# The second feed-forward product by 26 chained block products instead of two times seven

## The chip, the cores and the metric

The kernel runs on one core of a Trainium2 chip. The metric is the device time of one execution in microseconds (us). Three executions of the kernel before gave 2304.38, 2305.03 and 2305.79 us; the median, 2305.03, is the time before.

## What is computed

One layer of a decoder: 2048 tokens of width 1024, a mixer (gated linear attention beside dilated windowed attention), then a feed-forward block of width 4096, all in float32. The change touches only the feed-forward block:

```python
nm = rmsnorm(h, mlp_norm_g[l])
a = jnp.square(jax.nn.relu(jnp.einsum('bsd,df->bsf', nm, w_ff1[l])))
h = h + jnp.einsum('bsf,fd->bsd', a, w_ff2[l])
...
return rmsnorm(h, final_norm_g)
```

So `a` is 2048 x 4096, `w_ff2` is 4096 x 1024, and the product of the two, added to `h` and normalised, is the output.

## The kernel before, in words

**One float32 product on TensorE.** Each float32 operand is split into a high part in the matmul's type and a low part with the rest (`split`, L408 to L410: ScalarE copies the high part, VectorE subtracts it to give the low part). `mm3` (L63 to L66) then issues three matmuls of 128x128 by 512 columns: high by high, low by high, high by low.

**The first product (FF1).** `product1` and `prep1` work through 2 halves of the tokens x 16 groups of 256 columns x 7 block products. A job is 12 matmuls into one PSUM bank. `prep1(at + 2)` makes the split weight block for the job two further on, in a ring of four. L1253 and L1254 apply ReLU and square. After the seventh job of a group, four sums of blocks (L1279 to L1282) are made on VectorE, and seven tiles of 128x512 go to the DRAM buffer `actD`, in the form in which the second product wants them. Seven 512-column pieces per group (X, c11 to c22, s2, s4) live in a double-buffered accumulator `acc1`. The transposed, split activations of a half fill 14 slots (`hb`); near job 106 of 224 `reload` brings in those of the other half, two more VectorE and ScalarE passes per `hb` pair.

**The second product (FF2).** It uses the same scheme of 7 products of 2x2 blocks, once for each half of the tokens: 14 phases. A phase has four PSUM banks (one for each 128 tokens) and 8 steps; a step takes 2 chunks of 128 inner columns, 24 matmuls. `load_a` brings 1 MB of activations for two steps, `prep_a` splits a step's 128x1024 of them (ring of 3, two steps ahead). `load_b`/`prep_b` bring and split the weights, subtracting a second block first where the product wants a difference (L1374); eight split weight tiles are kept, so that both halves use them. `taken` (L1400) adds a finished bank into the running sums (L1414), which start as `h`, and `output` (L1384) normalises a finished row block: squares on ScalarE (L1389), a multiply on GpSimd (L1391), one on VectorE (L1394), the scale on ScalarE (L1395), and the store. In the last phase the last three steps run bank by bank (L1504 on), so that each bank can be put out while the next one is multiplied.

**What sets the order.** A framework schedules: it puts the instructions into a fixed order on each engine and waits in them by semaphores. An engine runs its own instructions in that order. Nearly all DMAs are issued by SyncE's queue (SP). All large tiles come from one pool of 25 slots of 128x2112 float32; a new tile waits until a slot is free. PSUM has eight banks, named a (2), c (3), d (2), o (1).

Of the kernel before, what the change touches and what calls it, by code (L numbers as in the profile page):

```python
# [18 lines left out]
D = 1024  # L19
# [18 lines left out]

def emit(tc, a, stop=99):
# [23 lines left out]
    def mm3(out, sh, sl, mh, ml, first, last):  # L63
        T.matmul(out, sh, mh, start=first, stop=False)  # L64
        T.matmul(out, sl, mh, start=False, stop=False)  # L65
        T.matmul(out, sh, ml, start=False, stop=last)  # L66
# [80 lines left out]
    actD = dram.tile([7, 2, FF // 256, 128, 512], F32, name="actD")  # L147
    tD = dram.tile([2, FF // 256, 128, 512], F32, name="tD")
# [996 lines left out]
    gs = slot("gs")  # L1145
    gM, gF = gs[:, :D], gs[:, D:2 * D]
# [92 lines left out]

    def product1(at):  # L1240
        g, j = jobs1[at]
        half, gh = divmod(g, NP)
        if not acc1:
            acc = [slot("acc1") for _ in range(4)]
            acc1.extend(t[:, 512 * q:512 * q + 512] for t in acc for q in range(4))
        X, c11, c12, c21, c22, s2, s4 = acc1[7 * (g % 2):7 * (g % 2) + 7]
# [9 lines left out]
        def store(q, n, v):  # L1256
            q.dma_start(actD[n - 1, half, gh], v)
# [3 lines left out]
        elif j == 2:  # L1261
            V.tensor_tensor(c11, p, X, op=OP.add)
            square(c11)
            store(A, 1, c11)
        elif j == 6:
            V.tensor_tensor(X, p, X, op=OP.add)
            V.tensor_tensor(c12, X, c22, op=OP.add)
        elif j == 3:
            V.tensor_tensor(c12, p, c12, op=OP.add)
            square(c12)  # L1270
        else:
            V.tensor_tensor(X, p, X, op=OP.add)
            V.tensor_tensor(c21, c21, X, op=OP.add)  # L1273
            V.tensor_tensor(c22, c22, X, op=OP.add)
            square(c22)
            square(c21)
            store(SP, 4, c22)
            store(SP, 2, c21)
            V.tensor_tensor(X, c12, c22, op=OP.add)  # L1279
            V.tensor_tensor(s2, X, c11, op=OP.subtract)  # L1280
            V.tensor_tensor(c12, c11, c12, op=OP.subtract)
            V.tensor_tensor(s4, c21, s2, op=OP.subtract)  # L1282
            for n, v in ((5, X), (6, s2), (7, c12), (3, s4)):
                store(SP, n, v)
# [39 lines left out]
    order2 = (1, 2, 5, 6, 3, 4, 7)  # L1324
    phases = [(j, half) for j in order2 for half in range(2)]
    raw_a, comb_a, raw_b, comb_b, sums = [], [], [], [], {}

# [4 lines left out]
    def load_a(n):  # L1332

        if n < 4 * len(phases):
            j, half = phases[n // 4]
            if len(raw_a) < 2:
                raw_a.append(view(slot("ra"), (4, 512)))
            SP.dma_start(raw_a[n % 2], actD[j - 1, half, 4 * (n % 4):4 * (n % 4) + 4].rearrange("c p s -> p c s"))

    def prep_a(n):  # L1340

        if n >= 8 * len(phases):
# [3 lines left out]
        c = comb_a[n % 3]  # L1346
        split(c[:, 0], c[:, 1], raw_a[n // 2 % 2][:, n % 2 * 2:n % 2 * 2 + 2])
# [3 lines left out]
    def load_b(n):  # L1351

        if n >= 56:
            return
        j, c = order2[n // 8], 2 * (n % 8)
        if len(raw_b) < 2:
            raw_b.append(view(slot("rb2"), (2, 2, 512)))
        pairs2 = tD.rearrange("k c p s -> k p c s")
        of = {(k, m): w2[:, 2 * c + k:2 * c + k + 3:2, 512 * m:512 * m + 512] for k in range(2) for m in range(2)}
        kept = [pairs2[k][:, c:c + 2] for k in range(2)]  # L1360
        for at, v in enumerate({1: [of[0, 0]], 2: [of[1, 0]], 5: [of[0, 1], of[0, 0]], 6: [of[1, 1], kept[0]],
                                3: [of[1, 1]], 4: [of[1, 0], kept[1]], 7: [of[1, 1], of[0, 1]]}[j]):
            SP.dma_start(raw_b[n % 2][:, at], v)

    def prep_b(n):

        if n >= 56:
            return
        j, c = order2[n // 8], 2 * (n % 8)
# [194 lines left out]
```

## Time and profile before

| what | value |
|---|---|
| median of three runs | 2305.03 us |
| span of the profiled execution, first to last instruction | 2300.5 us |
| TensorE busy (matmuls) | 2281.5 us, 99% of the span |
| VectorE / ScalarE / GpSimd busy | 1534.2 (67%) / 1182.0 (51%) / 308.2 us (13%) |
| DMA, mean over the span | 199 GB/s |

The profile gives no total of its own for the profiled execution beyond its span; the median of the runs lies 4.5 us above that span. In the rows, PE is TensorE's matmuls, PEld its weight loads, DVE is VectorE, ACT is ScalarE, POOL is GpSimd and SP is SyncE's DMA queue. A row of the groups has the line, engine, operation, output and inputs, shapes and count; then busy time in us and the mean ns of one; then the idle time of that engine just before such instructions and what ended it. Records of consecutive instructions on one engine overlap a little, so the distance between two starts is shorter than a duration: matmuls of 512 columns have records of 389 ns and start every 0.23 us.

### The profile page before, as it was taken

Reading aid. Unit: us, or ns where it says so; the run is one execution under the profiler, and the core shown is the slowest. Engines: PE = TensorE matmul, PEld = TensorE weight load, DVE = VectorE, ACT = ScalarE, POOL = GpSimd, SP = SyncE. Lnnn points to the kernel's source line nnn. Section 1 sums busy time; section 2 is a strip of 40 time slices with the busy share of each in tenths; the row PEclk is TensorE's granted clock in tenths of the full one; section 3 lists DMA queues with packets and bytes.
Section 4 is the critical chain, followed back from the end, with each engine's and each line's share of the span. In section 5 each row is a group of like instructions: output and inputs, shape, how many; then the busy total and the mean of one; then the engine's idle time right before and its main releaser. Section 6 shows DMA issues by size and latency. Waiting matters only on the chain.

```text
span 2300.5 us, 34940 instructions
## 1 busy us (share of the span) xinstructions
PE 2281.5 (99%) x12700; PEld 1976.2 (86%) x12700; DVE 1534.2 (67%) x2845; ACT 1182.0 (51%) x2372; POOL 308.2 (13%) x394
## 2 busy tenths in 40 slices
PE   9999999999999999999999999999999999999998
PEld 8978998899999988888888888888888888888887
DVE  7787867767767685446777788777755446447444
ACT  6665536426877783335555566555544323225224
POOL 1210002024476671000000000000000100000002
PEclk9999999999999999999999999999999999999999
DMA  6467745776768765678544456444487477448543
GB/s 209 124 197 240 252 138 157 210 234 222 230 196 255 239 218 166 201 254 264 190 151 151 151 190 240 151 151 151 151 279 253 160 263 265 144 158 287 193 161 110
DMA packets 341806, 457.60 MB, mean 199 GB/s; under 512 B 18118, under 2 KB 214231, under 8 KB 336257
## 3 DMA queue, kind: packets, MB, share of 16 engines
q1 hardware_dynamic: 336878, 446.71, 60.0%
q10 hardware_dynamic: 4754, 8.66, 1.0%
q8 instruction: 100, 1.64, 0.3%
q14 instruction: 74, 0.60, 0.1%
HBM read 292.99 MB, written 167.02 MB: 200 GB/s over the span
## 4 chain that ended last, share of the span: by engine, by line
PE 52%; ACT 1%; DVE 0%; issue 0%; ACTq 0%
PE ps_c L65 6%; PE ps_c L66 6%; PE ps_c L64 6%; PE ps_a L66 4%; PE ps_a L65 4%; PE ps_a L64 4%; PE ps_d L64 4%; PE ps_d L66 4%; PE ps_d L65 4%; PE ps_o L66 2%; PE ps_o L65 2%; PE ps_o L64 2%; ACT scr L1389 0%; DVE hb L410 0%; ACT hb L409 0%
## 5 line engine op out<-in xcount | busy, mean ns | idle before, releaser
L410 DVE TENSOR_TENSOR ca<-ra,ca 128x1024 fp32r<-128x1024 f32 x112 | 138.0, 1232 | 171.3 <-ACT ca L409 171.2
L409 ACT ACTIVATE ca<-ra 128x1024 fp32r<-128x1024 f32 x112 | 117.9, 1053 | 229.9 <-PE ps_c L66 191.1
L409 ACT ACTIVATE w1comb<-w1raw 128x512 fp32r<-128x512 f32 x224 | 140.0, 627 | 153.6 <-PE ps_c L66 56.1
L1391 POOL TENSOR_TENSOR suma<-suma,gs 128x512 f32<-128x512 f32 x16 | 23.4, 1477 | 1393.6 <-ACT scr L1389 1393.6
L410 DVE TENSOR_TENSOR w1comb<-w1raw,w1comb 128x512 fp32r<-128x512 f32 x224 | 153.8, 689 | 50.5 <-ACT w1comb L409 50.4
L816 PE MATMUL ps_a<-v,pt 128*128 128x65 f32 x1200 | 178.4, 253 | 2.5 <-ACT pt L804 1.8
L788 ACT ACTIVATE pe<-pe,O 128x256 f32<-128x256 f32 (+1 forms) x384 | 156.6, 453 | 46.3 <-DVE O L787 42.8
L816 PEld LDWEIGHTS ps_a<-v,pt 128*128 128x128 f32 x1200 | 175.2, 195 | 3.6 <-ACT pt L804 2.1
L797 PE MATMUL ps_d<-ident,pe 128*128 128x128 f32 x600 | 159.3, 279 | 0.0
L787 DVE CUSTOM_DVE_ANT_0 pe<-ps_c,nb 128x256 f32<-128x256 f32 (+1 forms) x384 | 126.2, 360 | 40.9 <-PE ps_d L797 18.3
L209 ACT ACTIVATE wcomb<-wraw 128x512 fp32r<-128x512 f32 (+2 forms) x119 | 90.0, 757 | 99.0 <-PE ps_a L65 32.7
L409 ACT ACTIVATE cb<-rb 128x1024 fp32r<-128x1024 f32 x56 | 59.4, 1060 | 150.6 <-PE ps_o L65 115.0
L65 PE MATMUL ps_c<-hb,w1comb 128*128 128x512 f32 x336 | 130.8, 389 | 0.4 <-DVE w1comb L410 0.4
L64 PE MATMUL ps_c<-hb,w1comb 128*128 128x512 f32 x336 | 130.7, 389 | 0.0
L66 PE MATMUL ps_c<-hb,w1comb 128*128 128x512 f32 x336 | 130.7, 389 | 0.0
L64 PE MATMUL ps_c<-cb,ca 128*128 128x512 f32 x336 | 130.7, 389 | 0.0
L65 PE MATMUL ps_c<-cb,ca 128*128 128x512 f32 x336 | 130.7, 389 | 0.0
L66 PE MATMUL ps_c<-cb,ca 128*128 128x512 f32 x336 | 130.7, 389 | 0.0
L410 DVE TENSOR_TENSOR cb<-rb,cb 128x1024 fp32r<-128x1024 f32 x56 | 68.2, 1222 | 64.6 <-ACT cb L409 64.6
L797 PEld LDWEIGHTS ps_d<-ident,pe 128*128 128x128 f32 x600 | 109.8, 187 | 0.1
L1253 ACT ACTIVATE acc<-acc 128x512 f32<-128x512 f32 x128 | 79.6, 631 | 51.3 <-DVE acc L1273 35.1
L64 PE MATMUL ps_a<-wo,mT 128*128 128x512 f32 x256 | 101.3, 396 | 0.0
(423 smaller groups left out, 7036.7 us busy)
## 6 DMA issues: line engine op xcount, KB each, us to landing
ra<-actD SPq DMA_DIRECT2D x56, 1024.0 KB, 6.5
actD<-acc SPq DMA_DIRECT2D x192, 256.0 KB, 2.5
rb<-w_ff SPq DMA_DIRECT2D x72, 512.0 KB, 4.8
w1raw<-w_ff SPq DMA_DIRECT2D x32, 1024.0 KB, 5.7
k<-kD SPq DMA_DIRECT2D x16, 1024.0 KB, 8.1
rb<-hTD SPq DMA_DIRECT2D x13, 1024.0 KB, 5.7
wraw<-w_in SPq DMA_DIRECT2D x48, 256.0 KB, 3.6
cmb<-boD SPq DMA_DIRECT2D x16, 528.0 KB, 7.3
```

What stands on the lines that cost most here:

```text
L64: T.matmul(out, sh, mh, start=first, stop=False)
L65: T.matmul(out, sl, mh, start=False, stop=False)
L66: T.matmul(out, sh, ml, start=False, stop=last)
L209: A.activation(hi, src, AF.Copy, scale=sc)
L409: A.activation(hi, src, AF.Copy)
L410: V.tensor_tensor(lo, src, hi.bitcast(F32), op=OP.subtract)
L787: V.tensor_tensor_reduce(p, s, bias, scale=1.0, scalar=BIG, op0=OP.add, op1=OP.min, accum_out=nm)
L788: A.activation(p, p, AF.Exp, bias=nm, scale=-1.0)
L797: T.transpose(pb[:, i * 128:i * 128 + 128], src, ident)
L816: T.matmul(self.b.opsum[:, n % 4], self.pt[:, i * 128:i * 128 + 128], self.b.v[:, blk, cols], start=first, stop=last)
L1253: A.activation(v, v, AF.Relu)
L1391: G.tensor_tensor(C[0], C[0], gF[:, :512], op=OP.mult)
```

## The change

FF2 becomes one bilinear scheme for a 4x4 grid of activation blocks (each 512 tokens x 1024 inner columns) by a 4x2 grid of weight blocks (1024 x 512): 26 products (`PRODUCTS`) in 26 phases of four steps. A line of `PRODUCTS` has the sign of the activations, the mark `c` of a chained product, the weight blocks (row and column of the grid, with `=`, `+` or `-`), and behind the bar the running sums to which the bank goes. A step is still 24 matmuls and 1 MB of activations for two steps.

- **Activations.** The 26 left operands are sums of 256-column blocks (`SUMS`). `act_sums` makes them in FF1 on GpSimd, 28 instructions of 128x256 for every two groups: 5 after the even group, 23 after the odd one. Four operands are plain blocks (`SINGLE`). The four VectorE sums L1279 to L1282 are gone, and so are the seven stores a group: now there are 11 stores of two sums and 4 of single blocks for every two groups, in rows of 1 KB instead of 2 KB. The accumulators are two tiles for even groups and one for odd groups.
- **Weights.** A running weight operand (`state`, two slots) is changed from product to product: a part marked `=` is loaded into it, others are loaded beside it (`fetch_b`, ring of four) and added or subtracted in place (`update_b`): the first of a product on GpSimd, a second on VectorE. `prep_b` splits it each step, in a ring of 3; nothing is kept for a second half.
- **Sums of products.** Two sets of four banks alternate (`held2`). A product marked `c` goes on accumulating in the banks of the product two phases before, after these have been read; where a sign is wanted, `prep_a` negates the activations. `taken` adds a bank to as many of the eight running sums as the right side lists. The running sums are loaded with `h` as their first phase begins (`begin`).

The core of the diff:

```diff
+SUMS = """14 = a00 + a02
+9 = a00 - a20
+16 = a12 + 14
+20 = a02 + a12
+t0 = a10 + 16
+13 = a31 - a30
+25 = a11 + a31
+4 = a21 + a23
+15 = a30 - 25
+17 = t0 + 15
+10 = a20 - a21
+8 = a00 - 10
+t1 = a03 + a13
+23 = a01 + t1
+24 = t1 + 8
+21 = a11 + 23
+t2 = a13 + a33
+7 = a23 + t2
+3 = a32 - t2
+5 = a21 + 7
+18 = a12 + 3
+6 = a30 + 5
+t3 = a01 + a03
+19 = t3 - 3
+t0 = a32 - 5
+t1 = a22 + t0
+11 = a02 - t1
+12 = a20 + t1"""
...
+PRODUCTS = """1 . =00 +01 | +11
+1 . =31 | -01 +11 -31
+1 . =20 +30 | -20 +30
+1 . +21 | +00 -10
+1 c +31 | +21
+1 c -01 -11 | +31
+-1 c =01 +11 | -31
+1 c -21 -31 | -21
+1 . +10 -30 | +01 +20
+-1 c +00 |
+1 . =01 -21 | +01
+-1 c =20 | +20
+1 c =21 | +21
+1 . =11 | +31
+1 . =21 | +01
+1 c =11 -00 | -30
+-1 c =00 +21 | -11
+1 c =00 | +10 -11
+1 c =20 +21 | +10
+1 . =30 | +00
+1 c =00 -20 | -00 -20
+-1 c =10 +11 | -01
+1 . =10 -30 | +00
+1 c +11 | +01 -10
+1 c -31 | -01
+1 c =00 +10 | +30"""
...
     mixD = dram.tile([S, D], F32, name="mixD")
     hD = dram.tile([S, D], F32, name="hD")
     hTD = dram.tile([2, 7, 128, 4, 512], F32, name="hTD")
-    actD = dram.tile([7, 2, FF // 256, 128, 512], F32, name="actD")
-    tD = dram.tile([2, FF // 256, 128, 512], F32, name="tD")
+    actD = dram.tile([NPH, 128, 8, 2, 256], F32, name="actD")
...
+    xs1, ring1, even, odd = [], [], [], []
+    def act_block(name, cs):
+        i, k = int(name[1]), int(name[2])
+        t, lo = divmod(i, 2)
+        return cs[k % 2][:, 2 * (k // 2) + t, 256 * lo:256 * lo + 256]
+    def act_sums(half, q, cs, which):
+        if not ring1:
+            ring1.extend([view(slot("ring1"), (8, 256)), view(xs1[0][:, 1024:], (4, 256))])
+        outs_, temps = ring1
+        for name, _, x, op, y in which:
+            at = MADE.index(int(name)) if name[0] != "t" else None
+            value = lambda v: (act_block(v, cs) if v[0] == "a" else temps[:, int(v[1])] if v[0] == "t"
+                               else outs_[:, MADE.index(int(v)) % 8])
+            dst = temps[:, int(name[1])] if at is None else outs_[:, at % 8]
+            G.tensor_tensor(dst, value(x), value(y), op=OP.add if op == "+" else OP.subtract)
+            if at is not None and at % 2:
+                SP.dma_start(actD[at - 1:at + 1, :, q, half].rearrange("r p s -> p r s"), outs_[:, at % 8 - 1:at % 8 + 1])
     def product1(at):
...
+        q, par = divmod(gh, 2)
+        if not xs1:
+            xs1.append(slot("xs1"))
+        cs = even if par == 0 else odd
+        if len(cs) < (2, 1)[par]:
+            cs.append(view(slot("acc1"), (4, 512)))
+        C4 = cs[q % len(cs)]
+        X = xs1[0][:, 512 * par:512 * par + 512]
+        c11, c12, c21, c22 = [C4[:, n] for n in range(4)]
+        both = (even[q % len(even)], C4)
...
+        def single(n):
+            for r, name in SINGLE.items():
+                if int(name[2]) % 2 == par and 2 * (int(name[2]) // 2) + int(name[1]) // 2 == n:
+                    SP.dma_start(actD[AT[r], :, q, half], act_block(name, both))
...
+            single(0)
...
+            single(1)
...
+            square(c21)
+            single(2)
             square(c22)
-            square(c21)
-            store(SP, 4, c22)
-            store(SP, 2, c21)
-            V.tensor_tensor(X, c12, c22, op=OP.add)
-            V.tensor_tensor(s2, X, c11, op=OP.subtract)
-            V.tensor_tensor(c12, c11, c12, op=OP.subtract)
-            V.tensor_tensor(s4, c21, s2, op=OP.subtract)
-            for n, v in ((5, X), (6, s2), (7, c12), (3, s4)):
-                store(SP, n, v)
+            single(3)
+            act_sums(half, q, both, SUMS[EARLY:] if par else SUMS[:EARLY])
...
+        if n < 2 * NPH:
+            p, k = divmod(n, 2)
...
+            SP.dma_start(raw_a[n % 2], actD[AT[p], :, 4 * k:4 * k + 4].rearrange("p q h s -> p q (h s)"))
...
+        c, r = comb_a[n % 3], raw_a[n // 2 % 2][:, n % 2 * 2:n % 2 * 2 + 2]
+        if PRODUCTS[n // 4][0] > 0:
+            split(c[:, 0], c[:, 1], r)
+        else:
+            A.activation(c[:, 0], r, AF.Copy, scale=-1.0)
+            V.scalar_tensor_tensor(c[:, 1], r, -1.0, c[:, 0].bitcast(F32), op0=OP.mult, op1=OP.subtract)
...
+    def w2_part(n, k, m):
+        first = 8 * (n % 4) + 2 * (k % 2) + k // 2
+        return w2[:, first:first + 5:4, 512 * m:512 * m + 512]
...
+    def fetch_b(n):
+        if n >= LAST:
...
+        if not raw_b:
+            raw_b.extend(view(v[:, 1024 * e:], (2, 512)) for v in [slot("rb2") for _ in range(2)] for e in range(2))
+        fetched[n] = []
+        for op, k, m in PRODUCTS[n // 4][2]:
+            if op != "=":
+                v = raw_b[turns[0] % 4]
+                turns[0] += 1
+                SP.dma_start(v, w2_part(n, k, m))
+                fetched[n].append((op, v))
+    def update_b(n, engines=(G, V)):
+        if n >= LAST:
+            return
+        v = state_of(n)
+        for op, k, m in PRODUCTS[n // 4][2]:
+            if op == "=":
+                SP.dma_start(v, w2_part(n, k, m))
+        for e, (op, r) in enumerate(fetched.pop(n)):
+            engines[e].tensor_tensor(v, v, r, op=OP.add if op == "+" else OP.subtract)
...
+        v = comb_b[n % 3]
+        split(v[:, 0], v[:, 1], state_of(n))
...
+        for (k, m), n in began.items():
+            if n == ph:
+                acc2[k, m] = view(slot("sum"), (4, 512))
+                for h in range(2):
+                    SP.dma_start(acc2[k, m][:, 2 * h:2 * h + 2],
+                                 h6[k // 2, k % 2, :, h, :, 512 * m:512 * m + 512])
...
+        for op, k, m in PRODUCTS[ph][3]:
+            v = acc2[k, m][:, i]
+            V.tensor_tensor(v, v, p, op=OP.add if op == "+" else OP.subtract)
+        for k, n in done_at.items():
+            if n == ph:
+                half, m = divmod(i, 2)
+                output([acc2[k, n][:, i] for n in range(2)], 1024 * half + 256 * k + 128 * m, i,
+                       ph == NPH - 1 and i == 3)
...
+        mm3(p, l[:, 0, c, tk], l[:, 1, c, tk], r[:, 0, c], r[:, 1, c], first and n % 4 == 0 and c == 0,
+            n % 4 == 3 and c == 1, skip_group_check=True)
...
+        n = at + 6 - len(jobs1)
+        if n == 0:
+            load_a(0)
+        if 0 <= n < 4:
+            fetch_b(n)
+            update_b(n, (V, V))
+        if n == 3:
+            load_a(1)
+        if n in (3, 5):
+            prep_b(n // 2 - 1)
+            prep_a(n // 2 - 1)
+            fetch_b(n // 2 + 3)
+    held2 = [None, None]
     left = None
...
+    for ph, (_, chained, _, _) in enumerate(PRODUCTS):
+        if not chained:
+            held2[ph % 2] = [ps(t) for t in ("acdc", "adco")[ph % 2]]
+        P = held2[ph % 2]
+        for k in range(4):
+            n = 4 * ph + k
+            update_b(n + 4)
+            if n + 6 not in fetched:
+                fetch_b(n + 6)
             prep_a(n + 2)
...
+            prep_b(n + 2)
+            if k == 1:
+                begin(ph)
+            if left:
                 taken(ph - 1, k, left[k])
...
+            if ph < NPH - 1 or k < 2:
                 for c in range(2):
                     for i in range(4):
...
+                        mm2(P[i], n, c, i, not chained)
         left = P
     for i in range(4):
...
+        for n in (LAST - 2, LAST - 1):
             for c in range(2):
...
+                mm2(left[i], n, c, i, False)
+        taken(NPH - 1, i, left[i])
     es.close()
```

163 lines of the change are left out of this document (47 added, 116 removed).

## The prediction

> **What bounds the kernel now.** I read the page's first parts, then busy time by stage, then the groups of FF1 and FF2, and last the instructions around each GpSimd multiply.
>
> ```profile
> span 2300.5 us, 34940 instructions
> ...
> PE 2281.5 (99%) x12700; PEld 1976.2 (86%) x12700; DVE 1534.2 (67%) x2845; ACT 1182.0 (51%) x2372; POOL 308.2 (13%) x394
> ...
> PEclk9999999999999999999999999999999999999999
> ```
> TensorE is busy nearly all the time, at the full granted clock. The stage table (stretch, length, busy time of PE, PEld, DVE, ACT, POOL, clock, DMA share, GB/s) says the same of both feed-forward stages:
>
> ```profile
> 1100.00:1688.00 588.00, 587.53 (x2592) 486.15 (x2591) 455.24 (x695) 339.43 (x569) 0.00 (x0) 1.00 0.51 170
> 1688.00:2276.00 588.00, 588.00 (x2596) 486.89 (x2595) 299.68 (x298) 197.17 (x268) 18.05 (x12) 1.00 0.62 209
> 2108.00:2150.00 42.00, 42.00 (x187) 34.77 (x186) 23.84 (x24) 17.59 (x31) 0.00 (x0) 1.00 0.82 287
> ```
> The first row lies in FF1, the second in FF2. FF2 has no idle time on TensorE: 588.00/2596 = 0.2265 us a matmul. VectorE is busy 51% there, ScalarE 34%, GpSimd 3%. In FF1 VectorE stands at 77%. So the kernel is bound by the number of matmuls, and fewer of them are worth their full price as long as the other engines stay under TensorE's time. The whole question is whether they do.
>
> **Part 1: the matmuls that go.** FF2 before is 14 phases x 8 steps x 24 = 2688 matmuls, after 26 x 4 x 24 = 2496. 192 fewer x 0.2265 = **-43.5 us**. A phase becomes 96 x 0.2265 = 21.7 us, a step stays 5.44 us. FF1 keeps its 2688, and two groups take 168 x 0.2265 = 38.05 us. Chaining in PSUM costs no matmul, since a chained product only leaves out the start flag. It takes a wait on the bank's reading by VectorE, two phases after the bank was begun and one after it was complete, so a phase of 21.7 us stands between.
>
> **Part 2: FF1, sums moved to GpSimd.** VectorE loses four instructions a group and GpSimd gains 28 for every two groups.
>
> ```profile
> L410 DVE TENSOR_TENSOR w1comb<-w1raw,w1comb 128x512 fp32r<-128x512 f32 x224 | 153.8, 689 | 50.5 <-ACT w1comb L409 50.4
> ...
> L1225 DVE TENSOR_TENSOR w1raw<-w1raw 128x512 f32<-128x512 f32 x32 | 22.2, 692 | 37.1 <-DMA w1raw<-w_ff 37.1
> ...
> L1281 DVE TENSOR_TENSOR acc<-acc 128x512 f32<-128x512 f32 x32 | 21.9, 685 | 0.0
> ```
> ```profile
> L946 POOL TENSOR_TENSOR gla<-gla 128x256 f32<-128x256 f32 x16 | 11.7, 732 | 0.1
> ```
> L1281 stands for the four lines that go, each 32 times: 4 x 21.9 = 88 us off VectorE, worth nothing by itself, since VectorE did not bound. L946 is the nearest row to a new GpSimd sum: 28 x 0.73 = 20.5 us in 38.05, or 54%. Alone that fits. But the two engines are not alone:
>
> ```profile
> 1815.46 1.96 DVE L410 TENSOR_TENSOR ca<-ra,ca 128x1024 fp32r<-128x1024 f32 x1 [0.47 <-ACT ca L409]
> ```
> ```profile
> 1816.30 2.27 POOL L1391 TENSOR_TENSOR suma<-suma,gs 128x512 f32<-128x512 f32 x1
> ```
> ```profile
> L410 DVE TENSOR_TENSOR ca<-ra,ca x112: 1211/1220/1957, 1672.5 to 2277.8; 128x1024 fp32r<-128x1024 f32 x112
> ```
> ```profile
> L1391 POOL TENSOR_TENSOR suma<-suma,gs x16: 1268/1302/2287, 1813.8 to 2294.5; 128x512 f32<-128x512 f32 x16
> ```
> A VectorE subtract that takes 1.22 us took 1.96 beside a GpSimd multiply, and the next multiply took 2.27 instead of 1.27, ending 1.15 us after the subtract did. They did not share, they took turns. VectorE instructions that read one input from PSUM (L1414, 0.68 us) show no such stretch beside the same multiplies. So I count turns: VectorE instructions with both inputs in SBUF, plus all GpSimd sums.
>
> In FF1 these are, per group, 7 splits, 4 weight sums (L1225 to L1230), L1267, L1273 and L1274: 14, so 28 for two groups. How long is a turn? Records overlap; in a stretch where VectorE runs without a pause:
>
> ```profile
> 1412.37 0.68 DVE L1282 TENSOR_TENSOR acc<-acc,acc 128x512 f32<-128x512 f32 x1
> ...
> 1416.58 0.68 DVE L1228 TENSOR_TENSOR w1raw<-w1raw 128x512 f32<-128x512 f32 x1
> ```
> eight starts, seven distances, 4.21/7 = 0.60 us each. Turns for two groups: 28 x 0.60 + 28 x 0.73 = 37.3 us of 38.05, or 98%. With whole records, 28 x 0.689 + 20.5 = 39.8 us. That is the narrow place of this change. The bounds are 0 (the turns just fit, and the four PSUM reads a group lie beside GpSimd) and, with whole records, (39.8 - 38.05) x 16 = 28 us. I take the distance, because it is measured back to back, and add a local loss near job 106, where the second half is reloaded:
>
> ```profile
> L410 DVE TENSOR_TENSOR hb<-rb,hb 128x1024 fp32r<-128x1024 f32 x14 | 16.7, 1214 | 0.0
> ```
> 14 splits, 17 us of turns, in some 30 us that have hardly any left. GpSimd may fall behind by about 10 us there before the single odd accumulator makes VectorE wait for it. I take **+6 us** for all of FF1.
>
> The Trainium skill, SBUF — State Buffer, section "Who interferes with whom", says that a VectorE instruction with two SBUF inputs and a GpSimd instruction reading SBUF exclude one another for the whole instruction. The trace agrees that they exclude one another (1.96 against 1.22 us); taken literally, the rule asks for the 39.8 us and so for +28 in place of +6.
>
> DMA issues in FF1: 15 stores for two groups instead of 14, all on SP, where two of the 14 were on ScalarE's queue. They wait there for GpSimd, and behind them waits `load_w1`, for which L1225 waits.
>
> ```profile
> actD<-acc SPq DMA_DIRECT2D x192, 256.0 KB, 2.5
> ...
> w1raw<-w_ff SPq DMA_DIRECT2D x32, 1024.0 KB, 5.7
> ```
> A weight load is asked for a group ahead (19 us) and takes 5.7, so a store may hold it back some 13 us unseen. The eight-piece ring of sums gives a store six GpSimd instructions (4.4 us) to land in, against 2.5; rows of half the length may cost some of that. I cost both at nothing; where that cover is gone, GpSimd is late, as in the third rival.
>
> **Part 3: FF2, more splits and sums.** Nothing is kept for a second half, so weights are split 104 times instead of 56, like the activations (112 before). Over FF2's 565 us:
>
> ```profile
> L410 DVE TENSOR_TENSOR ca<-ra,ca 128x1024 fp32r<-128x1024 f32 x112 | 138.0, 1232 | 171.3 <-ACT ca L409 171.2
> L409 ACT ACTIVATE ca<-ra 128x1024 fp32r<-128x1024 f32 x112 | 117.9, 1053 | 229.9 <-PE ps_c L66 191.1
> ```
> ```profile
> L1374 DVE TENSOR_TENSOR rb<-rb 128x1024 f32<-128x1024 f32 x32 | 39.2, 1224 | 45.3 <-DMA rb<-w_ff 45.2
> ...
> L1414 DVE TENSOR_TENSOR suma<-suma,ps_c 128x512 f32<-128x512 f32 x11 | 7.5, 682 | 0.0
> ```
> VectorE: 208 splits x 1.23 = 256, 12 second weight sums x 1.22 = 15, 33 targets x 4 banks x 0.68 = 90, 16 outputs x 0.75 (L1394 in the tail, below) = 12: 373 us, 66%. ScalarE: 208 x 1.05 + 16 outputs x 3.0 = 266 us, 47%. GpSimd: 19 products x 4 = 76 sums of 128x1024, twice the 1.27 of L1391 = 2.5 us each, 190, plus 16 x 1.27: 37%. All hidden on average. By step, two splits back to back take turns of 1.15 us (the distance of these starts):
>
> ```profile
> 1820.60 1.23 DVE L410 TENSOR_TENSOR cb<-rb,cb 128x1024 fp32r<-128x1024 f32 x1 [3.19 <-ACT cb L409]
> 1821.75 1.22 DVE L410 TENSOR_TENSOR ca<-ra,ca 128x1024 fp32r<-128x1024 f32 x1
> ```
> so 2 x 1.15 + 2.5 = 4.8 of 5.44 us. In products 5, 7 and 8 a second sum on VectorE makes it 6.0, over by 0.5 x 12 steps = 6 us; operands are made two steps (10.9 us) ahead, which covers most. VectorE's second sum waits for GpSimd's first, and splits and bank sums queue behind it: if nothing overlaps, a step is 6.0 + 0.6 = 6.6, over by 1.1 x 12 = 13 us. I take **+3** (0 to +13).
>
> DMA: 52 loads of 1 MB, 160 weight parts of 0.5 MB (72 before, with 32 more for the kept differences), 8 MB each of `h` and output: 155 MB in 565 us, 275 GB/s. A stretch of FF2 now moves 287 at a share of 0.82, so this fits, with longer queues.
>
> ```profile
> ra<-actD SPq DMA_DIRECT2D x56, 1024.0 KB, 6.5
> ...
> rb<-w_ff SPq DMA_DIRECT2D x72, 512.0 KB, 4.8
> ```
> A weight step is requested four steps (21.7 us) ahead: 4.8 load + 2.5 sum + 2.3 split = 9.6, cover of 12 us.
>
> **Part 4: the tail.**
>
> ```profile
> 2292.59 0.39 PE L66 MATMUL ps_o<-cb,ca 128*128 128x512 f32 x1
> ```
> ```profile
> 2293.74 0.63 ACT L1389 ACTIVATE scr<-suma 128x512 f32<-128x512 f32 x1 [0.51 <-DVE suma L1414]
> ...
> 2295.96 0.72 ACT L1395 ACTIVATE suma<-suma,stats 128x512 f32<-128x512 f32 x1
> 2296.71 0.35 ACTq L1398 DMA_DIRECT2D out<-suma  x1
> ```
> ```profile
> 2295.90 0.75 DVE L1394 SCALAR_TENSOR_TENSOR sumd<-sumd,stats,gs 128x512 f32<-128x512 f32 x1 [1.60 <-ACT stats L98]
> ```
> An output occupies ScalarE for 3.0 us (2293.74 to 2296.68). Before, the last banks came every 18 matmuls, 4.1 us. After, they come every 12, 2.7 us, and the product before also ends a row block, so ScalarE has 8 outputs (24 us) and 4 splits (4.2) in the last phase's 21.7 us. It ends 6.5 us plus a 0.7 us VectorE sum behind TensorE; with 3.8 us for the store, 11.0 against 7.5 now. I take **+3** (0 to +6).
>
> **Sum.** -43.5 + 6 + 3 + 3 = -31.5 us. The profiled span of 2300.5 becomes 2269; the 4.5 us by which the median lies above that span are kept: **2274 us**.
>
> **The rivals.**
> - *The turns cost whole records*: +28 instead of +6, 2296 us. For it: 39.8 us exceed 38.05. Against: the back-to-back distance of 0.60. Chance 0.18.
> - *FF2 waits for weights*, so that fewer matmuls do not become less time: +13 instead of +3, 2284, up to 2300 if DMA queues add to it. Against it: 12 us of cover. Chance 0.07.
> - *GpSimd is kept out, on the other side.*
>
> ```profile
> L274 POOL TENSOR_TENSOR acc<-acc,misc x32: 718/944/6267, 78.4 to 383.2; 128x264 f32<-128x264 f32 x16, 128x248 f32<-128x248 f32 x16
> ```
> One multiply that takes 0.72 us took 6.27 in an early stage where VectorE ran in a train. If GpSimd only gets VectorE's pauses, the next odd group's first sum must wait on VectorE until the odd accumulator has been read, and behind it wait the weight splits TensorE needs. At worst nothing of either engine lies beside the other, not even PSUM reads: 36 x 0.60 + 20.5 = 42.1 us for two groups, +4.0 x 16 = 65, so 2305 - 43.5 + 65 + 6 = 2332 us. It decides the sign from 40.4 us for two groups on ((43.5 - 6)/16 = 2.3 over 38.05). Against it: VectorE has 18 instructions a group instead of 22, hence more pauses. Chance of slower 0.19, with 0.06 for a halfway stop at no difference.
>
> **How the numbers follow.** The forecast, 2259 to 2283, has 0.50: the low end is all covers holding (2305 - 43.5 - 2 for reading errors), the high end FF1's reload and FF2's bounds together. With 0.18 and 0.07, faster has 0.75; same 0.06; slower 0.19. A measurement tells 0.2%, 4.6 us, from no change. The range is 2259 to 2312, which leaves out most of the slower case and little else.
>
> **What would show it.** Right: FF2's matmuls 2496 with 0.2265 us each and no idle time; FF1's 38.05 us for two groups kept, with GpSimd near 55 to 60% busy there and its mean sum well over 0.73 us. Wrong in FF1: TensorE idle behind `w1comb` L410, VectorE waiting for GpSimd on `acc1`. Wrong in FF2: TensorE waiting for `ca` or `cb`, ScalarE idle behind `bs`. Wrong in the tail: more than 11 us between the last matmul and the end.

## The result and the profile after

| | before | after |
|---|---|---|
| median, 4 runs each | 2304.70 us (2302.78 to 2305.79) | 2324.64 us (2321.99 to 2326.86) |
| span of the profiled execution | 2300.5 us | 2320.2 us |

The ratio is 1.0087, 95% interval 1.0072 to 1.0101: slower by 0.9%, 50 us above the forecast and outside its range of 2259 to 2312. The page's line of busy times:

```profile
PE 2255.3 (97%) x12508; PEld 1942.2 (84%) x12508; DVE 1646.2 (71%) x2777; ACT 1200.6 (52%) x2404; POOL 954.4 (41%) x914
```
The 192 matmuls are gone (12700 to 12508). TensorE is busy 26 us less, but the span grew: it waits now. Busy time by stage (length, PE, PEld, DVE, ACT, POOL, clock, DMA share, GB/s) shows where:

```profile
1090.00:1345.00 255.00, 251.22 (x1103) 206.13 (x1102) 178.39 (x243) 132.79 (x236) 162.83 (x173) 1.00 0.47 148
1345.00:1410.00 65.00, 56.30 (x229) 44.25 (x228) 54.92 (x60) 40.05 (x65) 43.02 (x41) 0.95 0.59 194
1410.00:1690.00 280.00, 274.72 (x1204) 225.16 (x1203) 192.84 (x259) 143.01 (x255) 186.58 (x200) 1.00 0.46 147
1690.00:1745.00 55.00, 49.83 (x215) 39.68 (x214) 39.40 (x41) 25.66 (x36) 23.22 (x23) 1.00 1.00 348
1745.00:1800.00 55.00, 38.84 (x154) 30.35 (x153) 34.08 (x26) 15.22 (x15) 38.22 (x21) 0.88 0.78 273
1800.00:2200.00 400.00, 399.91 (x1763) 330.31 (x1762) 284.25 (x251) 149.45 (x155) 140.30 (x48) 1.00 0.72 246
2200.00:2240.00 40.00, 36.62 (x154) 29.47 (x153) 39.62 (x23) 19.95 (x38) 33.42 (x13) 0.96 0.76 258
2240.00:2310.00 70.00, 68.67 (x302) 56.35 (x301) 57.30 (x50) 41.89 (x98) 40.77 (x18) 1.00 0.55 188
```
A record of a matmul lasts longer than its turn, so "busy" hides part of a gap. I measure TensorE's loss in a stretch as its length less its matmuls x 0.2265 us, and do so in all that follows. The loss holds gaps and slow matmuls alike: behind the gap of 12 us that is shown below, seven matmuls start 0.42 to 0.60 us apart instead of 0.2265 (granted clock 0.53 from 1755 to 1765), which is 1.6 us of the loss there. In order of the rows: 5.2, 13.1, 7.3 in the first product (FF1), where the same stretches before (1123, 285 and 1237 matmuls) lost 0.6, 0.4 and -0.2; then 6.3, 20.1, 0.7, 5.1, 1.6 in the second (FF2), which lost nothing before. So FF1 loses 24.8 us more, half of it in the reload stretch (1345 to 1410), and FF2 33.8, most of it at its start. The tail:

```profile
2310.93 0.39 PE L143 MATMUL ps_o<-cb,ca 128*128 128x512 f32 x1
```
From the end of the last matmul (2311.33) to that of the span it is 8.9 us against 7.5 before. -43.5 + 24.8 + 33.8 + 1.4 = +16.5 of the +19.7 by which the span grew; 3.2 us are not placed. The stretches begin at 1090, and each counts the matmuls that run across both its edges, so that one without a gap comes out at up to 0.5 us below nothing: the same five stretches of FF2 before come to -1.1 in sum.

Groups of after (busy us, mean ns | idle before and what ended it); L486 is the low half of `split`, L1333 the sums of activations, L1490 the weight sums:

```profile
L1490 POOL TENSOR_TENSOR bs<-bs,rb 128x1024 f32<-128x1024 f32 x72 | 215.1, 2995 | 290.8 <-DMA bs<-w_ff 230.7
...
L486 DVE TENSOR_TENSOR cb<-bs,cb 128x1024 fp32r<-128x1024 f32 x104 | 176.7, 1700 | 130.7 <-ACT cb L485 129.9
L486 DVE TENSOR_TENSOR w1comb<-w1raw,w1comb 128x512 fp32r<-128x512 f32 x224 | 178.8, 802 | 72.9 <-ACT w1comb L485 72.7
...
L1333 POOL TENSOR_TENSOR ring<-acc 128x256 f32<-128x256 f32 x80 | 74.0, 934 | 285.4 <-ACT acc L1357 261.6
```
Both engines take longer where they work at the same time: a split of FF1 goes from a mean of 689 to 802 ns, one of FF2 from 1232 to 1700, a GpSimd sum to 934 ns in this group (975 in all 448 sums) where the nearest row of before had 732, a weight sum to 3.0 us where I had counted 2.5.

In the reload stretch TensorE waits for such a split. Two rows of the list of waits there (us in total, times, longest):

```profile
POOL ring L1333 <- ACT acc L1357: 20.1, 3, 10.7
PE ps_c L142 <- DVE w1comb L486: 4.9, 2, 3.4
```
A split into `w1comb` takes 936 ns here in the mean (684 before in the same stretch), one into `hb` 1394 (1214 before). From 1395 to 1405 VectorE is busy 9.97 of 10 us and TensorE makes 16 matmuls. GpSimd is not behind: with a row of 4.2 us for `xs` it stands 24 us and waits for ScalarE's squares.

And the start of FF2, first SyncE's queue, then GpSimd, then ScalarE, then two stretches:

```profile
1714.79 2.79 SPq L1536 DMA_DIRECT2D sum<-hD  x4
...
1718.57 1.49 SPq L1536 DMA_DIRECT2D sum<-hD  x2
...
1725.42 9.77 SPq L1536 DMA_DIRECT2D sum<-hD  x7
```
```profile
1746.35 0.74 POOL L1333 TENSOR_TENSOR ring<-xs,ring 128x256 f32<-128x256 f32 x1 [12.54 <-DMA actD<-ring]
```
```profile
1751.29 1.06 ACT L485 ACTIVATE cb<-bs 128x1024 fp32r<-128x1024 f32 x1 [11.96 <-DMA bs<-w_ff]
...
1760.07 1.06 ACT L485 ACTIVATE cb<-bs 128x1024 fp32r<-128x1024 f32 x1 [0.57 <-POOL bs L1490]
```
```profile
1710.00:1749.00 39.00, 38.07 (x167) 30.91 (x166) 24.92 (x26) 16.27 (x21) 13.47 (x13) 1.00 1.03 368
1749.00:1765.00 16.00, 4.15 (x12) 2.95 (x11) 6.81 (x4) 5.18 (x5) 13.05 (x11) 0.68 1.02 386
```
All 16 loads of running sums (16 x 512 KB = 8 MB; the three that these rows leave out go at 1722 and 1737) are issued between 1714 and 1740, though `begin` asks for each only in the phase that first needs it: a load waits for nothing but its slot, and the framework sets it ahead. For 55 us the DMA engines are full (share 1.02 to 1.03). Two things come late by it. A weight part leaves at 1742.98, behind these loads, and lands 8 us later; ScalarE has waited 12 us for it. And GpSimd, still at FF1's last sums, waits 12.5 us until a store of its ring has landed; its first weight sum begins only at 1757.70. The split of that weight sum (1760.07) is what TensorE waits for at last: it has no matmul from 1749 to 1761.18, and 12 matmuls in the 16 us of the last row.

### The profile page after: what moved, and what is told of

Same layout as the page of the kernel before. It is cut to its first block, busy times and chain, and to the rows that moved or that the text cites. A ratio compares the mean times of both kernels' runs of the same rounds, so it can differ in the third digit from the quotient of the medians.

```text
span 2320.2 us, 35443 instructions
## 1 busy us (share of the span) xinstructions
PE 2255.3 (97%) x12508; PEld 1942.2 (84%) x12508; DVE 1646.2 (71%) x2777; ACT 1200.6 (52%) x2404; POOL 954.4 (41%) x914
## 4 chain that ended last, share of the span: by engine, by line
PE 64%; DVE 11%; DMA 10%; POOL 5%; ACT 5%; issue 4%; SPq 0%; DVEq 0%; ACTq 0%; POOLq 0%
PE ps_a L142 8%; PE ps_a L143 8%; PE ps_a L141 8%; DMA w1raw<-w_ff 6%; PE ps_c L142 5%; PE ps_c L143 5%; PE ps_c L141 4%; PE ps_a L892 4%; PE ps_o L143 3%; PE ps_o L142 3%; PE ps_o L141 2%; PE ps_d L873 2%; POOL ring L1333 2%; DVE w1comb L486 2%; PE ps_c L851 2%
## 5 line engine op out<-in xcount | busy, mean ns | idle before, releaser
L1490 POOL TENSOR_TENSOR bs<-bs,rb 128x1024 f32<-128x1024 f32 x72 | 215.1, 2995 | 290.8 <-DMA bs<-w_ff 230.7
L485 ACT ACTIVATE cb<-bs 128x1024 fp32r<-128x1024 f32 x104 | 110.1, 1059 | 316.0 <-issue 118.0
L486 DVE TENSOR_TENSOR cb<-bs,cb 128x1024 fp32r<-128x1024 f32 x104 | 176.7, 1700 | 130.7 <-ACT cb L485 129.9
L486 DVE TENSOR_TENSOR w1comb<-w1raw,w1comb 128x512 fp32r<-128x512 f32 x224 | 178.8, 802 | 72.9 <-ACT w1comb L485 72.7
L1333 POOL TENSOR_TENSOR ring<-acc 128x256 f32<-128x256 f32 x80 | 74.0, 934 | 285.4 <-ACT acc L1357 261.6
L350 POOL TENSOR_TENSOR acc<-acc,misc 128x264 f32<-128x264 f32 (+1 forms) x32 | 38.7, 1220 | 313.1 <-DMA wraw<-w_in 200.3
L486 DVE TENSOR_TENSOR ca<-ra,ca 128x1024 fp32r<-128x1024 f32 x84 | 119.9, 1431 | 6.1 <-ACT ca L485 6.1
L141 PE MATMUL ps_c<-cb,ca 128*128 128x512 f32 x312 | 122.4, 392 | 0.9 <-ACT acc L1365 0.7
L142 PE MATMUL ps_c<-cb,ca 128*128 128x512 f32 x312 | 122.4, 392 | 0.0
L143 PE MATMUL ps_c<-cb,ca 128*128 128x512 f32 x312 | 122.2, 392 | 0.0
L805 POOL CAST qp<-qs 128x512 fp32r<-128x512 f32 x64 | 68.9, 1161 | 121.3 <-DMA gkD<-acc 104.0
```

The lines of the kernel that those rows point to most:

```text
L141: T.matmul(out, sh, mh, start=first, stop=False, **kw)
L142: T.matmul(out, sl, mh, start=False, stop=False, **kw)
L143: T.matmul(out, sh, ml, start=False, stop=last, **kw)
L485: A.activation(hi, src, AF.Copy)
L486: V.tensor_tensor(lo, src, hi.bitcast(F32), op=OP.subtract)
L1333: G.tensor_tensor(dst, value(x), value(y), op=OP.add if op == "+" else OP.subtract)
```

## The experiments

Theory **P**: FF1's loss is the turns of GpSimd's sums with VectorE. Theory **Q**: the loss at FF2's start is the early loads of the running sums. Rivals: **W**, the weight loads of FF1 are late because they stand behind the stores of the sums in SyncE's queue; **N**, FF2 is simply short of engine time or DMA. Every ratio is to the kernel before, timed on the same chip. An added line moves the line numbers behind it.

**e1: running sums in program order**

```diff
-                    SP.dma_start(acc2[k, m][:, 2 * h:2 * h + 2],
-                                 h6[k // 2, k % 2, :, h, :, 512 * m:512 * m + 512])
+                    tc.keep_in_program_order(
+                        SP.dma_start(acc2[k, m][:, 2 * h:2 * h + 2],
+                                     h6[k // 2, k % 2, :, h, :, 512 * m:512 * m + 512]))
```


> One edit to the changed kernel: the loads of h into the running sums are kept in program order on SyncE's queue, so that each is issued when its first phase begins, and not all sixteen at the start of FF2. Theory Q (FF2's first 60 us lose 21 us, because 8.4 MB of running sums go out ahead of the weights and activations that the next steps need): that loss shrinks to 0 to 5 us, the total falls by 16 to 21 us to 2304 to 2309. Rival R (the loss there is GpSimd, late with the last sums of FF1, and weight sums queued behind them): the loss stays, within 4 us of 2324.6.

Measured: 2313.69 us (2312.03 to 2316.44), ratio 1.0047 [1.0032, 1.0062]; 11 us under the changed kernel. Its stages:

```profile
1745.00:1800.00 55.00, 54.58 (x242) 44.84 (x240) 49.96 (x41) 20.16 (x21) 34.92 (x16) 1.00 0.91 326
1800.00:2200.00 400.00, 394.32 (x1723) 323.51 (x1722) 279.10 (x241) 148.07 (x162) 140.43 (x48) 1.00 0.73 251
```
The 20.1 us of the first row are 0.2, and GpSimd's last sums, which rival R of the expectation blames, are still there: Q holds. But the second row now loses 9.7 instead of 0.7, so that part of the gain is given back. Most of it is lost from 1800 to 1825 (3.0) and from 1850 to 1900 (4.5), where VectorE makes the second weight sums of products 5, 7 and 8. They wait there for GpSimd's first sum, 20.5 us in all and 8.5 at the longest; in the changed kernel they wait 19.3 us, 2.3 at the longest, and TensorE loses nothing. Whether the spread loads bring the loss about is not shown.

**e2: sums of activations on VectorE**

```diff
-            G.tensor_tensor(dst, value(x), value(y), op=OP.add if op == "+" else OP.subtract)
+            V.tensor_tensor(dst, value(x), value(y), op=OP.add if op == "+" else OP.subtract)
```


> One edit to the changed kernel: the 28 activation sums of every two groups in FF1 run on VectorE instead of GpSimd. Theory P (FF1 loses 27 us because GpSimd and VectorE take turns): two groups take 38.1 to 38.5 us again, the loss of FF1 falls to under 6 us and the total by 18 to 25 us, to 2300 to 2307; VectorE gets 28 x 0.34 = 9.5 us more for two groups, 31 of 38. Rival W (FF1 loses because the weight loads of FF1 come late, behind stores that wait for sums): the stores still wait for sums, so most two-group times stay near 39.2 and the total stays within 6 us of 2324.6.

Measured: 2295.64 us (2292.78 to 2296.38), ratio 0.9965 [0.9952, 0.9978]: by this line alone the change is faster than before. FF1:

```profile
1090.00:1345.00 255.00, 254.62 (x1124) 210.51 (x1123) 217.31 (x430) 138.07 (x241) 0.00 (x0) 1.00 0.48 151
1345.00:1410.00 65.00, 61.09 (x261) 49.51 (x260) 61.19 (x108) 43.02 (x68) 0.00 (x0) 0.97 0.65 210
1410.00:1680.00 270.00, 270.00 (x1193) 223.58 (x1192) 230.88 (x462) 148.30 (x260) 0.00 (x0) 1.00 0.52 162
```
Losses 0.4, 5.9, -0.2. VectorE does all of its work and GpSimd's, and has 15% of its time left; in the reload stretch it is busy 94%, and that is what is left there. P holds. VectorE's waits for FF1's weights fall with it, from 95 to 41 us, so that this run alone does not rule out W; e7 tests that. FF1's 19.5 us (25.6 to 6.1) are most of the gain; the rest is in FF2.

**e3: no sums** (the 28 sums are left out; the ring is set to zero once and still stored, so 22 of the 26 left operands are zero)

```diff
+            V.memset(ring1[0], 0.0)
-            G.tensor_tensor(dst, value(x), value(y), op=OP.add if op == "+" else OP.subtract)
```


> The 28 GpSimd sums of every two groups in FF1 are left out; the ring that they fill is set to zero once and stored as before, so 22 of the 26 activation operands are zero. Theory P: GpSimd is idle in FF1, two groups take 38.1 us, total down by 22 to 27 us plus what FF2's start owed to late sums. Rival W: the same gain only if stores waiting for sums held up weight loads; if the loads are late for another reason, VectorE still waits for them and two groups stay over 39 us.

Measured: 2340.20 us (2336.50 to 2340.27), ratio 1.0157 [1.0142, 1.0172]. The expectation missed, by a cause that the experiment made. SyncE's queue, then three stretches:

```profile
1175.19 0.67 SPq L1285 DMA_DIRECT2D w1raw<-w_ff  x1
1175.90 22.81 SPq L1335 DMA_DIRECT2D actD<-ring  x26
...
1206.16 0.66 SPq L1285 DMA_DIRECT2D w1raw<-w_ff  x1
```
```profile
1165.00:1240.00 75.00, 50.51 (x204) 40.23 (x202) 28.30 (x42) 24.89 (x43) 0.00 (x0) 0.86 1.02 338
...
1340.00:1420.00 80.00, 80.00 (x355) 66.24 (x354) 52.39 (x78) 47.01 (x79) 0.00 (x0) 1.00 0.24 73
1420.00:1690.00 270.00, 269.77 (x1190) 223.12 (x1189) 179.37 (x267) 158.15 (x267) 0.00 (x0) 1.00 0.32 104
```
Stores that wait for nothing were all issued early, 26 of them between two weight loads, the DMA engines were full, and TensorE lost 28.8 us in the first row. The last of these stores goes at 1247; from 1240 to 1340 another 18.2 us are lost. From 1340 on nothing is (-0.4 and 0.5), the reload included: with P's sums away that stretch is free. The time says nothing about P, the last two rows do. The flood is Q's mechanism a second time.

**e4: e1 and e2 together**

> Both edits together: loads of h in program order, and the activation sums of FF1 on VectorE. If P and Q hold and do not overlap, the total falls by 34 to 46 us, to 2279 to 2291, below the kernel before (2304.7). If R or W holds, it stays above 2300.

Measured: 2286.91 us (2284.36 to 2289.13), ratio 0.9926 [0.9910, 0.9943], as P and Q together had it. FF1's reload stretch loses 6.8, and FF2 still loses, mostly here:

```profile
1800.00:2200.00 400.00, 392.41 (x1712) 321.52 (x1711) 282.77 (x238) 152.32 (x174) 148.43 (x52) 1.00 0.74 252
```
400 - 1712 x 0.2265 = 12.2 us, with VectorE at 71% and GpSimd at 37%: not short of engine time on average. In a group of this stage a VectorE split of weights takes 1647 ns and a GpSimd weight sum 2999.

**e5: e4 with the weight sums on VectorE too; e6: the output's multiply as well**

```diff
-    def update_b(n, engines=(G, V)):
+    def update_b(n, engines=(V, V)):
```
```diff
-                G.tensor_tensor(C[0], C[0], fin["g"][:, :512], op=OP.mult)
+                V.tensor_tensor(C[0], C[0], fin["g"][:, :512], op=OP.mult)
```


> This is the kernel with both edits (running sums loaded in program order, the 28 sums of activations on VectorE; 2286.9 us), and besides it every weight sum of the second product goes to VectorE: 72 GpSimd records of a mean 3.0 us become as many VectorE records of 1.2 us (the L1490 record that VectorE already has). VectorE then has 72 x 1.2 = 86 us more, about 470 to 500 of the 565 us of the second product. Theory T (what is left of the loss between 1745 and 2200, 16 us, is GpSimd's and VectorE's turns: a split of 1.2 us beside a weight sum takes 3.4): the splits fall to about 1.2 us, TensorE loses 4 to 8 us less, time 2279 to 2283. Rival D (the loads land late, whoever adds them): within 2 us of 2286.9. Rival B (VectorE becomes the bound in the phases with two-part weights, where it was 100% busy from 1784 to 1816): slower, 2290 to 2300.

> As e5, and besides it the output's multiplication by the final norm's gains is on VectorE (16 GpSimd records of 2.0 us become 16 of about 0.6 to 0.7), so that GpSimd does nothing in either feed-forward product. Theory T: the records of VectorE's own output step fall from 1.9 to about 0.7 us, the 5.9 us lost in phase 22 (around 2165 to 2190) shrinks to under 3, and the time is 2 to 4 us under e5. Rival B: the output steps bring 16 x 0.65 = 10 us more to VectorE in few phases, and phase 22 stays or grows; the time is that of e5 or up to 4 us above it.

Measured: e5 2282.91 us (2280.96 to 2286.27), ratio 0.9917 [0.9901, 0.9934]; e6 2281.40 (2280.10 to 2282.48), 0.9905 [0.9891, 0.9920]. Two stretches of e5, its splits, and what VectorE waits for in FF2:

```profile
1745.00:2000.00 255.00, 255.00 (x1126) 211.22 (x1125) 193.44 (x194) 94.76 (x94) 0.00 (x0) 1.00 0.76 263
2000.00:2200.00 200.00, 190.68 (x821) 154.14 (x820) 139.63 (x141) 77.52 (x101) 5.29 (x4) 0.99 0.73 245
```
```profile
L486 DVE TENSOR_TENSOR cb<-bs,cb 128x1024 fp32r<-128x1024 f32 x93 | 114.2, 1228 | 53.1 <-ACT cb L485 53.1
```
```profile
DVE bs L1490 <- DMA bs<-w_ff: 74.6, 27, 5.4
```
The splits are back at 1.23 us and the first stretch loses nothing. But the second loses 14.0, in phases that were clean: VectorE, in order, now stands before a weight sum until its load has landed (74.6 us in all), with the splits that TensorE needs queued behind. The time is in theory T's range, but T had not seen that most of what is gained early (e4 made 1084 matmuls in the first stretch and lost 9.5 us) is paid back late. e6's 1.5 us lie within the spread of the two. Its output records on VectorE are as short as T has it (0.74 us, 1.07 in e5), but from 2125 to 2200 both lose 9.8 us (288 matmuls), so nothing was won around the place that T named.

**e7: FF1's weight loads on ScalarE's queue** (from the changed kernel)

```diff
-            SP.dma_start(raw1[g % 2], w1[:, :, g0:g0 + 256])
+            A.dma_start(raw1[g % 2], w1[:, :, g0:g0 + 256])
```


> The changed kernel (2324.6 us) with one edit: the loads of the first product's weights are issued by ScalarE, so that they no longer stand behind the ring stores in SyncE's queue; GpSimd's sums stay. Theory P (the turns of GpSimd and VectorE cost the first product its 27 us): the pairs of groups with a loss keep it, 27 us falls by at most 6, time 2319 to 2325. Rival W (the weight loads are late because SyncE waits in front of a store for GpSimd's sum, as VectorE's 95 us of waits for w1raw would have it): the loss goes from 27 us to under 10, time 2305 to 2310.

Measured: 2320.25 us (2318.20 to 2323.18), ratio 1.0075 [1.0060, 1.0090].

```profile
1090.00:1345.00 255.00, 254.45 (x1121) 209.84 (x1120) 186.38 (x242) 134.46 (x237) 173.00 (x179) 1.00 0.47 147
1345.00:1410.00 65.00, 54.54 (x216) 42.73 (x215) 56.38 (x60) 40.44 (x63) 43.56 (x39) 0.92 0.58 187
1410.00:1690.00 280.00, 275.29 (x1206) 225.23 (x1204) 201.03 (x258) 141.87 (x253) 193.48 (x204) 1.00 0.48 151
```
Losses 1.1, 16.1, 6.8: FF1 as a whole goes from 25.6 to 24.0, although VectorE's waits for weights fall from 95 to 62 us. W explains little of FF1 as a whole. In the first stretch (5.2 in the changed kernel) it may be true, but the size is uncertain: e1, whose FF1 is that of the changed kernel, lost 7.4, 12.7 and 9.1 in the three stretches, so one trace is good to 2 or 3 us here.

**e8, e9, e10: what makes the splits of e6 late?** Theory Q2: they stand behind a weight sum that waits for its load. e8 emits the sums behind the step's splits; e9 asks for the first operand two steps earlier; e10 does both. (In e8 and e10 a fetch may overwrite a second operand before it is added, so some weight sums hold other blocks; the number and size of the instructions are the same.)

```diff
 # e8
-            update_b(n + 4)
+            load_b(n + 4)          # the part marked "=", taken out of update_b
             if n + 6 not in fetched:
                 fetch_b(n + 6)
             prep_a(n + 2)
             prep_b(n + 2)
+            update_b(n + 4)
 # e9: update_b stays first; at the end of prep_b
+        load_b(n + 4)
```


> As e6 (2281.4 us; it loses 14.2 us between 2010 and 2190, where VectorE stands 77 us in all before its weight sums until the load of the other operand has landed, and TensorE waits for the split of the activations queued behind), with the weight sums of a step emitted behind that step's two splits; the loads stay where they were. Theory Q2 (the splits are late because they stand behind a weight sum that waits for a load): 8 to 13 of the 14.2 us go, time 2269 to 2274. Rival D (VectorE has too much to do in those phases): within 2 us of 2281.4, the loss moves to other phases.

> As e6, with the load of the first weight operand (the one that is not a sum) asked for as soon as its buffer is free, two steps earlier, some 11 us; the weight sums stay where they were. Theory Q2: the wait of 77 us before the weight sums falls under 30 us, and 8 to 14 of the 14.2 us go: 2268 to 2274. Rival (the transfers themselves are what is slow, 260 to 350 GB/s in the slices around 2000): the wait stays above 60 us and the time within 3 us of 2281.4.

> Both of e8 and e9. Theory Q2: the second product has no loss above 2 us, and the time is that of the better of the two, or up to 3 us below it: 2267 to 2272, of which the reload stretch still loses 7 to 8. Rival: no better than e6, 2279 to 2284.

Measured: e8 2283.63 us (2280.74 to 2285.46), ratio 0.9911 [0.9896, 0.9926]; e9 2280.85 (2277.88 to 2284.34), 0.9901 [0.9886, 0.9916]; e10 2281.47 (2280.63 to 2282.70), 0.9904 [0.9887, 0.9920]. Theory Q2 missed in all three, and the rivals' figures were met, but for 0.2 us in e8 (VectorE's wait in e9 is still 73.2 us). The trace shows that the reasons were others. VectorE and SyncE's queue in e9 (the sums are L1495 there):

```profile
2114.68 1.22 DVE L486 TENSOR_TENSOR cb<-bs,cb 128x1024 fp32r<-128x1024 f32 x1
2115.81 1.22 DVE L486 TENSOR_TENSOR ca<-ra,ca 128x1024 fp32r<-128x1024 f32 x1
2121.05 1.22 DVE L1495 TENSOR_TENSOR bs<-bs,rb 128x1024 f32<-128x1024 f32 x1 [4.02 <-DMA bs<-w_ff]
2122.19 1.22 DVE L486 TENSOR_TENSOR cb<-bs,cb 128x1024 fp32r<-128x1024 f32 x1
```
```profile
2115.92 0.37 SPq L1487 DMA_DIRECT2D bs<-w_ff  x1
```
The load goes out as soon as the split frees its buffer (2115.92), but the next instruction of VectorE behind these two splits is already the sum that waits for a load, and it starts 5.1 us after this one went out. The framework had moved the sum ahead of the next splits, wherever the program had put it: in e8 and e10 too the sums are followed by the splits, and VectorE waits 80.8 and 77.8 us before them. So the runs had not changed what the theory was about. Moved program text is not a moved instruction.

**e11: the sums kept behind the splits**

```diff
 # e9, and
-            update_b(n + 4)
-            if n + 6 not in fetched:
-                fetch_b(n + 6)
             prep_a(n + 2)
             prep_b(n + 2)
+            update_b(n + 4)
+            if n + 6 not in fetched:
+                fetch_b(n + 6)
 # in update_b
-            engines[e].tensor_tensor(v, v, r, ...)
+            tc.keep_in_program_order(engines[e].tensor_tensor(v, v, r, ...))
```


> As e9 (2280.9 us), with the weight sums of a step behind its two splits in program order and kept there (in e9 the framework still set each sum ahead of the splits: the load is asked for at 2115.92 us, VectorE stands before the sum until 2121.05, and the split of the activations follows at 2123.33), and the fetch of the next sum operand behind them. Theory Q2 in its second form (the order on VectorE, not the load's time, makes the splits late): the gaps of TensorE between 2010 and 2190 go from 12.6 us to under 5, time 2270 to 2275. Rival F (the later fetch makes the sums' other operand late instead): the loss stays or moves to phases 0 to 8, time 2279 to 2290.

Measured: 2271.11 us (2270.14 to 2272.89), ratio 0.9859 [0.9843, 0.9876]; the fastest of all, and faster than before by 1.4%. VectorE, then two stretches:

```profile
2114.89 1.23 DVE L486 TENSOR_TENSOR cb<-bs,cb 128x1024 fp32r<-128x1024 f32 x1 [1.94 <-ACT cb L485]
2116.03 1.22 DVE L1496 TENSOR_TENSOR bs<-bs,rb 128x1024 f32<-128x1024 f32 x1
2117.17 1.22 DVE L486 TENSOR_TENSOR ca<-ra,ca 128x1024 fp32r<-128x1024 f32 x1
```
```profile
1730.00:1745.00 15.00, 13.04 (x51) 10.34 (x50) 13.45 (x18) 5.02 (x5) 0.00 (x0) 0.89 0.90 332
1745.00:2260.00 515.00, 515.00 (x2273) 426.43 (x2273) 397.09 (x410) 216.69 (x296) 0.00 (x0) 1.00 0.74 251
```
The sum no longer waits (2.6 us before all of the weight sums, 73.8 in e9). FF2 loses 3.4 us in the first row and 0.2 in the other 515 us. Q2 holds in its second form, and N falls: FF2 has the engine time and the DMA that it needs (VectorE busy 397 of 515 us, DMA share 0.74).

**e12: e11 with the first weight sum of a step on GpSimd again**

```diff
-    def update_b(n, engines=(V, V)):
+    def update_b(n, engines=(G, V)):
```


> As e11 (2271.1 us, no loss above 0.3 us in the second product after 1750), with the first weight sum of every step back on GpSimd, as in the changed kernel. Theory T (GpSimd's and VectorE's turns in the second product cost TensorE time by themselves, whatever the order): VectorE's splits go from 1.22 us to a mean of 1.5 to 1.7, and TensorE loses 8 us or more again between 1690 and 2240: 2279 or more. Rival S (the order was the cause; with it mended, VectorE's share of 0.83 leaves room for the turns): within 3 us of 2271.1.

Measured: 2278.67 us (2276.36 to 2281.54), ratio 0.9889 [0.9872, 0.9905]; 7.6 us above e11.

```profile
L486 DVE TENSOR_TENSOR cb<-bs,cb 128x1024 fp32r<-128x1024 f32 x102 | 165.7, 1624 | 119.5 <-ACT cb L485 119.4
```
```profile
1745.00:1800.00 55.00, 55.00 (x237) 45.33 (x236) 52.87 (x43) 19.61 (x20) 38.27 (x13) 0.97 0.76 260
1800.00:2200.00 400.00, 397.30 (x1749) 327.71 (x1748) 299.03 (x245) 155.42 (x178) 141.69 (x49) 1.00 0.75 254
```
It loses 1.3 and 3.9 us where e11 lost 0.2 in all; from 1690 to 2240 its losses are 9.1, those of e11 2.8. This is T's figure within 0.3 us of the time: order and turns are two causes. The trace also has about 2 us more than e11's in FF1's reload stretch, which this edit does not touch.

## Why the prediction was wrong, point by point

- **Part 1 (-43.5 us): right.** 2496 matmuls, and where nothing is late they start every 0.2265 us (1800 to 2200: 0.7 us lost of 400). With the edits of e11 the change is worth 2303.66 - 2271.11 = 32.6 us. That this is near the 31.5 forecast is luck in part, since the terms against it are others: FF1's 7, FF2's 4 and the tail's 1, in a kernel that leaves GpSimd out of both products.
- **Part 2 (+6): mis-sized; it measured +24.8.** The turns were the right mechanism (e2: 6.1 us are left when GpSimd is out). Their length for two plain groups was not far off: 5.2 us lost in the first stretch, 1.1 in e7. What failed is the "local loss near job 106": 13.1 us, not some 6, and 7.3 more behind it, which e2 removes as well. Its path failed too. "GpSimd may fall behind by about 10 us there before the single odd accumulator makes VectorE wait for it" does not happen: GpSimd waits 24 us for ScalarE in that stretch, and no wait of VectorE for GpSimd is listed in FF1. VectorE itself is slowed (936 ns a split instead of 684), has no pause where TensorE stands longest (busy 9.97 of 10 us), and TensorE waits for `w1comb`, one of the signs that the prediction had listed under "Wrong in FF1". "I cost both at nothing", of SyncE's queue, may have failed as well: e7 puts that at 1.6 us for FF1 as a whole, which one trace does not settle.
- **The rival with whole records (+28)** came near in sum, 24.8, and not in place: it asked for the same 1.75 us of every two groups, 11.7 us in the first stretch, which lost 5.2. That its sum came near is luck. It took the rule of the Trainium skill (SBUF — State Buffer, "Who interferes with whom") literally, by which such instructions of VectorE and GpSimd exclude one another. The traces agree that they lengthen one another (802 against 689 ns), but half of the loss sits in the reload stretch.
- **Part 3 (+3): the step that failed worst; it measured +33.8.** "155 MB in 565 us, 275 GB/s", "so this fits, with longer queues" was an average over the stage. 8 MB of it came at once, and "cover of 12 us" is of no use to a load that stands behind 8 MB: 20.1 us lost from 1745 to 1800, 0.2 in e1. (The 6.3 ahead of it go only with both edits: e1 makes 205 matmuls there and loses 8.6, e2 169 and loses 16.7, e4 from 1680 on 284 and loses 0.7. So they belong to Part 2 as much.) The rival "FF2 waits for weights" named the wait, at +13 and 0.07, but not its cause. The check by step (4.8 us of turns in 5.44) held in the changed kernel's middle (0.7 us lost), though with longer records than it had (1.70 and 3.0 us). In the phases with two weight sums (the term of +3, 0 to +13) the changed kernel loses nothing, e1 7.5 us. The 5.1 us at 2200 to 2240 fall where VectorE is busy 39.62 of 40 us, with outputs, splits and turns; which of them decides was not taken apart.
- **Part 4 (+3): right in sign, +1.4.**
- **The slower rival** had the sign, for another reason. FF1 lost 25 us, not 65, and VectorE's long waits there, in the list of waits of after from 1090 to 1710 (us in total, times, longest), are for weights and not for the odd accumulator:

```profile
DVE w1raw L1300 <- DMA w1raw<-w_ff: 95.3, 28, 5.9
```
FF1 alone (24.8) would have left the change faster, and so would FF2 alone (33.8). Neither of the two decided the sign; their sum did, and the forecast had priced each rival with all other terms at their forecast.

Still open: the 3.4 us that e11 loses around 1740, where DMA is at a share of 0.90; what e1's losses in the phases with two weight sums come from; what a part of FF1's loss owes to SyncE's queue; and whether the reload stretch could be relieved, which wasn't tried.

## What to carry to other kernels

Check a transfer budget for the worst 50 us, not for the stage: find each load and store that waits for nothing, since this scheduler sent them all at once, ahead of those that were needed (the running sums here, the stores in e3). An idle GpSimd is no free engine: moving its sums to a VectorE that then had 15% left was worth 29 us here (19.5 in FF1). Before an experiment on order is believed, read in the trace that the order changed.

## What the runs showed of the hardware that was not expected

A GpSimd sum of 128x1024 float32 took 3.0 us in the mean in FF2, and the splits on VectorE averaged 1.62 to 1.70 us (single ones up to 3.4) instead of the 1.23 of e5, where no weight sum is on GpSimd; the same sum took VectorE 1.22. With the DMA engines full (share 1.02), SyncE needed 0.88 us for each issue of the ring's store (26 in 22.81, in e3); in the changed kernel the median issue of this store took 0.36. After TensorE's gap of 12 us the next seven matmuls started 0.42 to 0.60 us apart instead of 0.2265, and after the gaps around 1400 in the reload stretch twelve came 0.43 us apart (granted clock 0.56 from 1405 to 1410): these gaps cost 1.6 and about 2.5 us beyond their own length.
